# Weight splits and rotation tables on the Vector engine, squares of queries and keys summed on the Scalar engine

## The chip, the cores and the metric

The kernel runs on one core of one Trainium2 chip. The core has a matrix engine (PE), a Vector engine (DVE), a Scalar engine (ACT), a GpSimd engine (POOL) and a sync engine (SP) that issues the DMAs here. The metric is the device time of one execution in microseconds (us). Three runs of the kernel before gave a median of 1289.25 us (1287.78 to 1290.65).

## The reference, cut to what matters

Two layers work on 512 latent tokens and 256 context tokens of width 1024. Layer 0 is a pooling mixer and a squared-ReLU MLP, layer 1 is grouped-query attention (8 query heads, 4 key and value heads of width 128) and again an MLP. The change lies between the MLP of layer 0 and the attention of layer 1.

```python
def qkv_proj(h, w_qkv, q_g, k_g):
    B, L, _ = h.shape
    qkv = h @ w_qkv
    q, k, v = jnp.split(qkv, [N_HEADS * HEAD_DIM, (N_HEADS + N_KV_HEADS) * HEAD_DIM], axis=-1)
    q = rms_norm(q.reshape(B, L, N_HEADS, HEAD_DIM), q_g)
    k = rms_norm(k.reshape(B, L, N_KV_HEADS, HEAD_DIM), k_g)
    v = v.reshape(B, L, N_KV_HEADS, HEAD_DIM)
    return q, k, v

def attn_mix(h_ctx, h_lat, w_qkv, w_o, q_g, k_g, ctx_out):
    B, S, _ = h_lat.shape
    qc, kc, vc = qkv_proj(h_ctx, w_qkv, q_g, k_g)
    ql, kl, vl = qkv_proj(h_lat, w_qkv, q_g, k_g)
    tables = axial_rope_tables(S)
    ql = apply_axial_rope(ql, tables)
    kl = apply_axial_rope(kl, tables)
    ...
```

Each query and key head is divided by the root of the mean of its 128 squares (`rms_norm`), times a gain, and the latent ones are rotated by tables of cosines and sines. The kernel multiplies the gains into the tables once.

## The kernel before

**Numbers in two parts.** A matmul here takes a value as a rounded high part and a low part that holds the rest. `hilo` (L85) makes both: ACT copies the source into the high part (L86), and another engine subtracts that from the source into the low part (L87). A product is then three matmuls per block. `load_w` (L141) brings a 128x1024 block of weights into a buffer `raw` by a DMA on SP's queue and splits it into a tile `w` by `hilo`; its argument `lo_eng` says which engine makes the low part, DVE if nothing is given. The pool of `raw` has two buffers and the pool of `w` four, so a load waits until the split of the load two before has read its buffer, and a split waits until PE has done with the tile four before.

**The stage around the change.** The MLP of layer 0 ends in `m2_chunk` calls (L471): for each of 8 blocks of the width PE sums six matmuls (L490) in a PSUM tile `mm` (2 buffers) or `aux` (4 buffers), and DVE adds it, times a gate, to the stream `h_lat` (L348). The context comes first, then the two halves of the latent tokens; behind each part the squares of the stream are summed (L263, L266 on ACT, L267 on DVE), and PE, DVE (L284) and POOL (L286) make of them the factor 1/rms, which PE spreads (L297) and ACT copies (L304). `modulated` (L307) then gives the normalised input `a_m` (latent) and `a_c` (context) in two parts: DVE multiplies (L315), ACT or DVE scales and shifts (L319, L321), and `hilo` splits.

`ahead` (L839) loads the first two key weights `w_6335` and `w_6340` before the last blocks of the MLP are out; L999 loads the other two. The tables are four products `tabs` on POOL (L1007) of `angles` and `grow`, which come by DMA into two `raw` buffers.

For each of six tiles of 128 tokens (two of the context, four latent), `k_tile` (L886) multiplies the keys on PE (`project`, L860, 24 matmuls of 512 columns), then takes `inv_rms` (L862): ACT squares the PSUM tile (L865, 128x512), DVE sums each head (L867) and scales (L868), POOL raises to -0.5 (L870). `rotated` (L873) forms the rotated keys on DVE from PSUM and the tables (L879, L881, L883), DVE multiplies by the result of POOL (L898), PE turns the tile (L902), and `hilo` stores it as `k`. `q_steps` (L911) does the same for the queries, two tiles at a time with its own transpose (L926). Two of these come before the values (`v_tile`, L906) and six inside the attention loop (L1038), beside scores, softmax and the products with values and output weights.

**Order.** A scheduler places the instructions of each engine in one fixed row; an engine takes its own in that order and waits at the first that is not ready.

Of the kernel before, what the change touches and what calls it, by code (L numbers as in the profile page):

```python
# [10 lines left out]
AF = mybir.ActivationFunctionType  # L11
ALU = mybir.AluOpType
AX = mybir.AxisListType

P = 128
# [4 lines left out]
T = SEQ + CTX  # L20
# [3 lines left out]
HD = 128  # L24
# [23 lines left out]
def dit_block_kernel(ctx: ExitStack, tc: tile.TileContext, xT, cols, adab, adaw, w1, w2, wqkv, wo,  # L48
                     poolw, gvec, rope, edge, eye, out):
    nc = tc.nc  # L50
    act, dve, pool, pe = nc.scalar, nc.vector, nc.gpsimd, nc.tensor
# [22 lines left out]
    def new(p, shape, dt, tag, bufs=None):  # L74
        uid[0] += 1
        kw = {"bufs": bufs} if bufs else {}
        return p.tile(shape, dt, tag=tag, name=f"{tag}{uid[0]}", **kw)
# [7 lines left out]
    def hilo(hi, lo, src, lo_eng=dve):  # L85
        act.activation(hi, src, AF.Copy)  # L86
        lo_eng.tensor_tensor(lo, src, hi.bitcast(F32), op=ALU.subtract)  # L87
# [53 lines left out]
    def load_w(src, lo_eng=dve, ring=None, raw=None):  # L141

        t = new(wp, [P, 2, 1024], F32R, "w")
        if raw is None:
            raw = new(*(ring or (raws, [P, 1024], F32, "raw")))
            nc.sync.dma_start(raw, src)
        hilo(t[:, 0], t[:, 1], raw, lo_eng)
        return t
# [97 lines left out]
    def new_m(name, ctx_too=True):  # L246

        parts = [[big.tile([P, KT, SEQ], F32R, tag=t, name=f"{name}_{t}") for t in ("m_hi", "m_lo")]]
        if ctx_too:
            parts.append([[mc.tile([P, 4, CTX], F32R, tag="mc", name=f"{name}_c{x}{i}") for i in range(2)] for x in range(2)])  # L250
        return parts
# [87 lines left out]
    def run(*steps):  # L339
        steps = list(steps)  # L340
        while steps:
            step(steps)
# [14 lines left out]
    def m1_chunk(ws, outs, m, groups):  # L357

        n = max(c + n for rs in groups for c, n in rs)
        pss = []  # L360
        for _ in range(0, len(ws), 1024 // n):
            ps = ps_mm()
            pss.extend(ps[:, i * n : i * n + n] for i in range(1024 // n))
        for ranges in groups:
            for w, ps in zip(ws, pss):
                for k in range(KT):
                    for wx in range(2):
                        lhs = w[:, wx, k * P : k * P + P]
                        for ax in range(2 - wx):
                            for c0, cn in blocks_of(ranges):  # L370
                                pe.matmul(ps[:, c0 : c0 + cn], lhs, ms(m, ax, k, c0, cn),  # L371
                                          start=k + wx + ax == 0, stop=k == KT - 1 and wx == 1)
        m1_done(outs, pss)
# [123 lines left out]
    def mlp(i, m, total, last, first=None, between=None, ahead=None, strassen=None, acts=(), ws=()):  # L497
        gate = mod[i][:, 40:48]
        prev, acts, sides = None, list(acts), []
        for c in range(NCH):  # L500
            w2s = ()
            if prev is not None and 5 <= c < NCH - 1:
                w2s = [load_w(w2[i, 2 * c - 2 + t]) for t in range(2)]
            if not acts:
                several = 2 if first and c == 0 else 1
                acts = [new(ap_, [P, 2, 2, T], F32R, "act") for _ in range(several)]
                if strassen and c > 1 and c >= strassen[0]:
                    raw = strassen[2]()
                    for t in range(2):
                        nc.sync.dma_start(raw[:, t], w1[i, 2 * c + t])  # L510
                    m1_strassen(raw, inputs, acts[0], strassen[3], m if total > SEQ else None)
                    ws = ()
                else:
                    ws = ws or [load_w(w1[i, 2 * c + t]) for t in range(2 * several)]
                outs = [a[:, t] for a in acts for t in range(2)]
                if not ws:
                    pass
                elif several > 1:
                    m1_chunk(ws, outs, m, first)
                else:  # L520
                    for t in range(2):
                        m1_chunk(ws[t : t + 1], outs[t : t + 1], m, [[(0, total)]])
                ws = ()
            a = acts.pop(0)
            if between:
                between(c)
            if c == NCH - 1:
                break
            if strassen and c == 1:
                strassen = strassen(m)  # L530
                inputs, sides = strassen[1]
            if prev is not None:
                side = [sides.pop(0)] if sides else []
                m2_chunk(w2s or [load_w(w2[i, 2 * c - 2 + t]) for t in range(2)], prev, gate, [(0, total)], side)
                run(*side)
            prev = a

        wa, wb = ([load_w(w2[i, 2 * c + t]) for t in range(2)] for c in (NCH - 2, NCH - 1))
        (rng, each, after), rest = last[0], last[1:]
        m2_chunk(wa, prev, gate, [rng])  # L540
        m2_chunk(wb, a, gate, [rng], each=each)
        side = []
        m2_chunk(wa, prev, gate, [(rest[0][0][0], sum(r[1] for r, _, _ in rest))], side, [after], 2)
        if ahead:
            ahead()
        after = ()
        for n, (rng, each, then) in enumerate(rest):
            m2_chunk(wb, a, gate, [rng], side, after, each=each)
            after = [then]
        run(*side)  # L550
        return after
# [117 lines left out]
    for dt in range(8):  # L669
# [3 lines left out]
        if dt == KT - 1:  # L673
            ws = [load_w(w1[0, t]) for t in range(2)]
# [16 lines left out]
    m = new_m("m")  # L691

    units = [u for k in range(0, KT, 2) for u in ((0, k, 1), (0, k + 1, 1), (1, k, 2))]
    act0 = new(ap_, [P, 2, 2, T], F32R, "act")
# [40 lines left out]
    for u in range(len(units) + 2):  # L735
# [7 lines left out]
        if u == 1:  # L743
            last = ada0_products(9)
# [3 lines left out]
    ws = [load_w(w1[0, 2 + t]) for t in range(2)]  # L748
# [47 lines left out]
    def to_attn(c0, n):  # L796
        def place():
            if c0 not in spot:
                if c0 == SEQ:
                    spot[c0] = new(mc, [P, 2, 2, n], F32, "mc")  # L800
                else:
                    t = new(ap_, [P, 4, 2, n], F32, "act")
                    spot[0], spot[256] = t[:, :2], t[:, 2:]
            return spot[c0]

        def each(dt):
            if dt % 2:
                squares(place()[:, 0] if dt > 1 else None, dt - 1, 2, c0, n, place()[:, 0])

        def after():  # L810
            yield from norm_steps(1, 0, c0, n, lazy_m("a", True), place()[:, 0], place()[:, 1, 0])
        return (c0, n), each, after()

    last = [to_attn(SEQ, CTX), to_attn(0, 256), to_attn(256, 256)]
    kws = []
# [20 lines left out]
            return tile_of  # L836
        return STRASSEN_FROM[0], strassen_inputs(m, xs, (opp, "op"), (0, 1, 3)), lambda: new(rawp, [P, 2, 1024], F32, "pair"), op

    norm = mlp(0, m, T, last, between=between0, strassen=strassen0, acts=[act0], ws=ws, ahead=lambda: kws.extend(load_w(wqkv[u], pool) for u in range(2)))  # L839
    am_ = lazy_m("a", True)  # L840


# [7 lines left out]
    tabs = big.tile([P, 4, 4, HD], F32, tag="h_ctx", name="tabs")  # L850
# [11 lines left out]
    def inv_rms(x, n):  # L862

        sq = new(sc, [P, n, HD], F32, "sc")
        act.activation(sq, x, AF.Square)  # L865
        ss = new(sm, [P, n], F32, "sm8")
        dve.tensor_reduce(ss, sq, axis=AX.X, op=ALU.add)  # L867
        dve.tensor_scalar(ss, ss, 1.0 / HD, EPS, op0=ALU.mult, op1=ALU.add)  # L868
        rr = new(sm, [P, n], F32, "rr", 4)
        pool.tensor_tensor(rr, ss, neghalf[:, :n], op=ALU.pow)  # L870
        return rr
# [124 lines left out]
        return norm_steps(1, 1, c0, n, lazy_m("m2", False), bank=c0 > 0)  # L996

    TILES = (4, 5, 0, 1, 2, 3)
    ws = kws + [load_w(wqkv[u], (dve, pool)[u % 2]) for u in range(2, 4)]  # L999
    angles = new(raws, [P, 2, 4, HD], F32, "raw")  # L1000
    nc.sync.dma_start(angles, rope)
    grow = new(raws, [P, 4, HD], F32, "raw")
# [1 line left out]
    gk = const.tile([P, HD], F32, tag="gk", name="gk")  # L1004
    nc.sync.dma_start(gk, gvec[:, 2])
    for x in (2, 3, 0, 1):
        pool.tensor_tensor(tabs[:, x], angles[:, x % 2], grow[:, x].unsqueeze(1).to_broadcast([P, 4, HD]), op=ALU.mult)  # L1007
    def q_fill(g, ws):
        return [q_steps(ws, half, (g, half)) for half in range(2)]

# [8 lines left out]
            step(norm)  # L1019
    run(ks[4])  # L1020
    prev = ks[5]
    fill = q_fill(0, [load_w(wqkv[8 + u], pool) for u in range(2)])
    ws = []
    for n in range(2):
        next(fill[n])
        next(fill[n])
        run(prev)
        next(fill[n])
        prev = fill[n]
        ws.extend(load_w(wqkv[4 + 2 * n + u], pool) for u in range(2))  # L1030
    st, late, pend, wos = {}, [], [], None
    for n, tt in enumerate(TILES):
        v_tile(ws, tt)
# [3 lines left out]
    fill = []  # L1037
    for n in range(8 * NKV):  # L1038
        g, half, i = n // 8, n // 4 % 2, n % 4
        if i == 0 and half == 0 and g + 1 < NKV:  # L1040
            fill = q_fill(g + 1, [load_w(wqkv[8 + 2 * (g + 1) + u], pool) for u in range(2)])
# [22 lines left out]
        if i == 3:  # L1064
            prev, fill = fill[:1], fill[1:]
# [114 lines left out]
```

## Time and profile before

| | us |
|---|---|
| median of three runs | 1289.25 |
| the profiled execution, its own time | 1293.01 |
| its span in the profile | 1291.2 |
| PE busy in the span | 1247.2 (97%) |
| DVE busy | 1031.4 (80%) |
| ACT busy | 578.4 (45%) |
| POOL busy | 292.0 (23%) |

The profile records each instruction with its start and length, and what an idle engine waited for. Matmuls overlap and their ends are modelled, so the busy share of PE says when it had work, not how fast it was; the granted clock says that. Instructions on one engine overlap at their ends by some hundredths of a microsecond. Idle time of an engine that nobody waits for costs nothing.

### The profile page before, as it was taken

To read this page: it belongs to the slowest core of one execution; us is meant where nothing else is said; L and a number is where in the kernel's file an instruction comes from. 1 tells how busy PE (TensorE), PEld (TensorE's weight loads), DVE (VectorE), ACT (ScalarE), POOL (GpSimd) and SP (SyncE) were. 2 spreads that over 40 slices of the span, in tenths; PEclk is the share of its full clock that TensorE was granted. 3 is DMA by queue.
4 is the path that set the end of the run, shared out by engine and by line. 5 is a ranking of instruction groups with operands and counts; after the bars stand their busy time and mean duration, and the time that the engine had idled before them with its cause. 6 is when DMAs were issued, how large, how long until landed. Compare 5 with 4: busy or idle time off the path is not lost. (4 is left out here: it accounts for less than half of the span.)

```text
span 1291.2 us, 20478 instructions
## 1 busy us (share of the span) xinstructions
PE 1247.2 (97%) x8150; PEld 1107.8 (86%) x8150; DVE 1031.4 (80%) x1681; ACT 578.4 (45%) x954; POOL 292.0 (23%) x213
## 2 busy tenths in 40 slices
PE   6999999999999999999988999999989999999997
PEld 5567888899999999999877799999978898989896
DVE  6564998878989888766888377888889889898976
ACT  5445523444344443443343254545554544445443
POOL 0000000122221222230135122211030434343412
PEclk8999999999999999999989999999999999999998
DMA  9666414333434333302011011102213322222111
GB/s 349 268 254 220 139 66 159 104 114 115 147 115 147 117 128 117 129 34 66 33 58 66 33 66 34 65 34 66 82 66 114 131 98 98 99 98 99 66 34 66
DMA packets 41312, 138.68 MB, mean 107 GB/s; under 512 B 4736, under 2 KB 8064, under 8 KB 41088
## 3 DMA queue, kind: packets, MB, share of 16 engines
q1 hardware_dynamic: 41216, 137.36, 30.4%
q8 instruction: 64, 1.05, 0.3%
q14 instruction: 32, 0.26, 0.1%
HBM read 135.25 MB, written 2.10 MB: 106 GB/s over the span
## 5 line engine op out<-in xcount | busy, mean ns | idle before, releaser
L490 PE MATMUL aux<-act,w 128*128 128x512 f32 (+1 forms) x1224 | 240.0, 347 | 3.2 <-DVE h_lat L348 3.1
L490 PE MATMUL mm<-act,w 128*128 128x512 f32 (+1 forms) x1224 | 239.2, 347 | 0.6 <-DVE act L383 0.6
L490 PEld LDWEIGHTS aux<-act,w 128*128 128x128 f32 x1224 | 195.7, 189 | 32.7 <-DVE h_lat L348 3.9
L490 PEld LDWEIGHTS mm<-act,w 128*128 128x128 f32 x1224 | 196.2, 190 | 32.1 <-issue 1.7
L86 ACT ACTIVATE w<-raw 128x1024 fp32r<-128x1024 f32 x106 | 109.9, 1054 | 126.1 <-PE aux L490 90.7
L428 POOL TENSOR_TENSOR sc<-pair 128x512 f32<-128x512 f32 x55 | 77.7, 1422 | 320.6 <-DVE h_lat L348 107.5
L348 DVE SCALAR_TENSOR_TENSOR h_lat<-aux,mod,h_lat 128x512 f32<-128x512 f32 (+1 forms) x204 | 125.4, 628 | 16.5 <-PE aux L490 14.6
L428 POOL TENSOR_TENSOR sc<-fin 128x512 f32<-128x512 f32 x60 | 96.2, 1619 | 172.7 <-DVE r L448 83.6
L87 DVE TENSOR_TENSOR w<-raw,w 128x1024 fp32r<-128x1024 f32 x87 | 108.0, 1256 | 27.9 <-ACT w L86 27.5
L348 DVE SCALAR_TENSOR_TENSOR h_lat<-mm,mod,h_lat 128x512 f32<-128x512 f32 (+1 forms) x140 | 96.5, 697 | 6.7 <-PE mm L490 5.2
L371 PE MATMUL mm<-m_m_hi,w 128*128 128x512 f32 (+1 forms) x320 | 93.9, 356 | 1.0 <-ACT m_m_hi L86 1.0
L860 PE MATMUL aux<-w,a_m_hi 128*128 128x256 f32 (+1 forms) x384 | 88.2, 325 | 0.0
L219 DVE SCALAR_TENSOR_TENSOR mc<-raw,s_f,mc 128x512 f32<-128x512 f32 x112 | 83.4, 764 | 2.1 <-DMA raw<-in_dram 1.4
L439 PE MATMUL mm<-m_m_hi,mc 128*128 128x256 f32 x384 | 71.0, 283 | 0.0
L87 POOL TENSOR_TENSOR w<-raw,w 128x1024 fp32r<-128x1024 f32 x19 | 47.1, 2494 | 99.5 <-ACT w L86 99.5
L860 PEld LDWEIGHTS aux<-w,a_m_hi 128*128 128x128 f32 x384 | 64.7, 194 | 5.4
L371 PEld LDWEIGHTS mm<-m_m_hi,w 128*128 128x128 f32 x320 | 57.4, 194 | 11.2 <-ACT m_m_hi L86 1.2
L459 PE MATMUL aux<-m_c,w 128*128 128x256 f32 x528 | 65.2, 283 | 0.0
L459 PEld LDWEIGHTS aux<-m_c,w 128*128 128x128 f32 x528 | 64.2, 192 | 0.0
L467 DVE TENSOR_TENSOR act<-r,act 128x512 fp32r<-128x512 f32 x46 | 48.2, 1048 | 19.7 <-ACT r L466 19.7
L860 PE MATMUL aux<-w,a_m_lo 128*128 128x256 f32 (+1 forms) x192 | 62.1, 323 | 0.0
L439 PEld LDWEIGHTS mm<-m_m_hi,mc 128*128 128x128 f32 x384 | 60.7, 192 | 0.5
(245 smaller groups left out, 2575.1 us busy)
## 6 DMA issues: line engine op xcount, KB each, us to landing
raw<-in_dram SPq DMA_DIRECT2D x157, 512.0 KB, 3.3
praw<-in_dram SPq DMA_DIRECT2D x34, 512.0 KB, 8.0
fin<-in_dram SPq DMA_DIRECT2D x24, 512.0 KB, 4.1
pair<-in_dram SPq DMA_DIRECT2D x22, 512.0 KB, 4.3
block<-in_dram SPq DMA_DIRECT2D x8, 512.0 KB, 6.0
h_lat<-in_dram SPq DMA_DIRECT2D x4, 512.0 KB, 7.0
w<-in_dram SPq DMA_DIRECT2D x4, 512.0 KB, 11.7
out_dram<-fin SPq DMA_DIRECT2D x8, 256.0 KB, 2.5
```

The costliest lines, as they stand in the source:

```text
L86: act.activation(hi, src, AF.Copy)
L87: lo_eng.tensor_tensor(lo, src, hi.bitcast(F32), op=ALU.subtract)
L219: dve.scalar_tensor_tensor(acc[:, s], w, scal, acc[:, s], op0=ALU.mult, op1=ALU.add)
L348: dve.scalar_tensor_tensor(h, ps, gate[:, dt, s : s + 1], h, op0=ALU.mult, op1=ALU.add)
L371: pe.matmul(ps[:, c0 : c0 + cn], lhs, ms(m, ax, k, c0, cn), start=k + wx + ax == 0, stop=k == KT - 1 and wx == 1)
L428: pool.tensor_tensor(t, x, y, op=how)
L439: pe.matmul(places[n], w[:, wx, k * P : k * P + P], inputs[n][ax][:, k], start=k + wx + ax == 0, stop=k == 3 and wx == 1)
L459: pe.matmul(pc[:, t * 256 : t * 256 + 256], ws[k // 4][:, wx, k % 4 * P : k % 4 * P + P], ms(m, ax, k, SEQ, CTX), start=k + wx + ax == 0, ...
L467: dve.tensor_tensor(lo, r, hi.bitcast(F32), op=ALU.subtract)
L490: pe.matmul(ps, lhs, a[:, t, ax, c0 : c0 + n], start=t + wx + ax == 0, stop=t == 1 and wx == 1)
L860: pe.matmul(ps, lhs, ws[u][:, wx, o : o + width], start=k + ax + wx == 0, stop=k == KT - 1 and ax == 1)
```

## The change

Four calls of `load_w` lose their argument `pool`, so that DVE makes the low parts of nine weight blocks in this stage: two key weights in `ahead`, one of the two in L999 (the other was with DVE already), two query weights and four value weights. The four products of the tables go from POOL to DVE. In `inv_rms` the one squaring of 128x512 and the sum over each head on DVE give way to four squarings of 128x128 on ACT, each with an accumulator output that gives the sum of its head; this holds for all 14 tiles of keys and queries. The split of the weights in the attention loop stays where it was, in part on POOL. From L867 on the numbers of the lines are those of before; L867 is now the squaring.

```diff
-    norm = mlp(0, m, T, last, ..., ahead=lambda: kws.extend(load_w(wqkv[u], pool) for u in range(2)))
+    norm = mlp(0, m, T, last, ..., ahead=lambda: kws.extend(load_w(wqkv[u]) for u in range(2)))
...
     def inv_rms(x, n):
         sq = new(sc, [P, n, HD], F32, "sc")
-        act.activation(sq, x, AF.Square)
         ss = new(sm, [P, n], F32, "sm8")
-        dve.tensor_reduce(ss, sq, axis=AX.X, op=ALU.add)
+        for i in range(n):
+            act.activation(sq[:, i], x[:, i], AF.Square, accum_out=ss[:, i : i + 1])
         dve.tensor_scalar(ss, ss, 1.0 / HD, EPS, op0=ALU.mult, op1=ALU.add)
...
-    ws = kws + [load_w(wqkv[u], (dve, pool)[u % 2]) for u in range(2, 4)]
+    ws = kws + [load_w(wqkv[u]) for u in range(2, 4)]
...
     for x in (2, 3, 0, 1):
-        pool.tensor_tensor(tabs[:, x], angles[:, x % 2], grow[:, x].unsqueeze(1).to_broadcast([P, 4, HD]), op=ALU.mult)
+        dve.tensor_tensor(tabs[:, x], angles[:, x % 2], grow[:, x].unsqueeze(1).to_broadcast([P, 4, HD]), op=ALU.mult)
...
-    fill = q_fill(0, [load_w(wqkv[8 + u], pool) for u in range(2)])
+    fill = q_fill(0, [load_w(wqkv[8 + u]) for u in range(2)])
...
-        ws.extend(load_w(wqkv[4 + 2 * n + u], pool) for u in range(2))
+        ws.extend(load_w(wqkv[4 + 2 * n + u]) for u in range(2))
```

Three places show how DVE's row changes. The first is DVE at the end of the MLP of layer 0, where the last block of 512 tokens (`aux_6327`) is added and the blocks of 256 follow (`mm_6345` is the first of them); before:

```order
L348 SCALAR_TENSOR_TENSOR h_lat<-aux_6327,mod_134,h_lat 128x512
L348 SCALAR_TENSOR_TENSOR h_lat<-mm_6345,mod_134,h_lat 128x256
L87 TENSOR_TENSOR a_c_6250<-sc_6313,a_c_6248 128x512
L348 SCALAR_TENSOR_TENSOR h_lat<-mm_6353,mod_134,h_lat 128x256
L348 SCALAR_TENSOR_TENSOR h_lat<-aux_6363,mod_134,h_lat 128x256
```

The same place on DVE in the changed kernel:

```order
L348 SCALAR_TENSOR_TENSOR h_lat<-aux_6327,mod_134,h_lat 128x512
L87 TENSOR_TENSOR w_6335<-raw_6336,w_6335 128x1024
L87 TENSOR_TENSOR a_c_6250<-sc_6313,a_c_6248 128x512
L87 TENSOR_TENSOR w_6340<-raw_6341,w_6340 128x1024
L348 SCALAR_TENSOR_TENSOR h_lat<-mm_6345,mod_134,h_lat 128x256
L348 SCALAR_TENSOR_TENSOR h_lat<-mm_6353,mod_134,h_lat 128x256
```

Two splits of key weights now stand between the last large block and the first small one. The second place is DVE where the first key tiles meet the norm of the second half of the latent tokens (`sm_6599`, in the changed kernel `sm_6601`, is its variance); before:

```order
L315 TENSOR_TENSOR sc_6524<-h_lat,act_6361 128x512
L867 TENSOR_REDUCE sm_6586<-sc_6584 128x4
L87 TENSOR_TENSOR a_m_lo<-sc_6518,a_m_hi 128x2x256
L321 TENSOR_SCALAR sc_6524<-sc_6524,am_139,mod_135 128x256
L868 TENSOR_SCALAR sm_6586<-sm_6586 128x4
L897 TENSOR_TENSOR sc_6591<-aux_6559,gk 128x512
L87 TENSOR_TENSOR a_m_lo<-sc_6524,a_m_hi 128x2x256
L898 TENSOR_TENSOR sc_6591<-sc_6591,rr_6589 128x512
L284 TENSOR_SCALAR sm_6599<-mm_6594 128x2
L897 TENSOR_TENSOR sc_6638<-aux_6606,gk 128x512
```

The same place on DVE in the changed kernel:

```order
L315 TENSOR_TENSOR sc_6524<-h_lat,act_6361 128x512
L87 TENSOR_TENSOR w_6544<-raw_6545,w_6544 128x1024
L87 TENSOR_TENSOR a_m_lo<-sc_6518,a_m_hi 128x2x256
L321 TENSOR_SCALAR sc_6524<-sc_6524,am_139,mod_135 128x256
L284 TENSOR_SCALAR sm_6601<-mm_6596 128x2
L87 TENSOR_TENSOR a_m_lo<-sc_6524,a_m_hi 128x2x256
L1007 TENSOR_TENSOR tabs<-raw_6549,raw_6551 128x512 x4
L868 TENSOR_SCALAR sm_6585<-sm_6585 128x4
L897 TENSOR_TENSOR sc_6593<-aux_6559,gk 128x512
L898 TENSOR_TENSOR sc_6593<-sc_6593,rr_6591 128x512
```

The variance of the second half (L284) now comes ahead of the first key tile instead of inside it, a split stands ahead of it and the four tables behind it. The third place is DVE in the key tile of the latent tokens 256 to 383 (its product is `aux_6757`, in the changed kernel `aux_6765`); before:

```order
L879 TENSOR_TENSOR sc_6796<-aux_6757,tabs 128x512
L881 TENSOR_TENSOR sc_6797<-aux_6757,tabs 128x4x64 x2
L883 TENSOR_TENSOR sc_6796<-sc_6796,sc_6797 128x512
L898 TENSOR_TENSOR sc_6796<-sc_6796,rr_6794 128x512
L867 TENSOR_REDUCE sm_6837<-sc_6835 128x4
```

The same place on DVE in the changed kernel:

```order
L879 TENSOR_TENSOR sc_6806<-aux_6765,tabs 128x512
L881 TENSOR_TENSOR sc_6807<-aux_6765,tabs 128x4x64 x2
L87 TENSOR_TENSOR w_6868<-raw_6869,w_6868 128x1024
L883 TENSOR_TENSOR sc_6806<-sc_6806,sc_6807 128x512
L87 TENSOR_TENSOR w_6873<-raw_6874,w_6873 128x1024
L898 TENSOR_TENSOR sc_6806<-sc_6806,rr_6804 128x512
```

The splits of the two query weights came in between the steps of the tile, and the reduction went. Behind the attention every engine's row is as before, and so is SP's row from the first instruction to the last.

## Rows read from the trace of the kernel before

**Rows 1.** Busy time of the engines in two stretches, the stage of the change and the attention loop (columns: stretch and its length; busy us and instructions of PE, PE's weight loads, DVE, ACT, POOL; granted clock; DMA).

```profile
630.00:720.00 90.00, 77.14 (x433) 66.75 (x432) 75.46 (x114) 36.09 (x56) 40.66 (x27) 0.94 0.20 68
720.00:920.00 200.00, 195.15 (x1427) 182.57 (x1426) 151.35 (x319) 94.80 (x181) 34.73 (x29) 1.00 0.13 43
```

**Rows 2.** Timeline of PE in the stage (start, length, instruction; in brackets the idle time ahead of it and who ended it).

```profile
632.45 2.32 PE L490 MATMUL aux<-act,w 128*128 128x256 f32 x18
...
637.84 0.38 PE L490 MATMUL aux<-act,w 128*128 128x256 f32 x1 [3.08 <-DVE h_lat L348]
638.24 0.98 PE L490 MATMUL mm<-act,w 128*128 128x256 f32 x6
...
653.77 2.79 PE L860 MATMUL aux<-w,a_c 128*128 128x512 f32 x11 [1.16 <-DVE w L87]
...
657.21 5.29 PE L860 MATMUL aux<-w,a_c 128*128 128x512 f32 x22
...
667.09 1.23 PE L297 MATMUL mm<-ident,sm 128*128 128x128 f32 x4 [3.23 <-POOL sm L286]
...
695.64 0.63 PE L902 MATMUL aux<-ident,sc 128*128 128x128 f32 x4 [2.62 <-DVE sc L898]
...
703.81 0.63 PE L902 MATMUL aux<-ident,sc 128*128 128x128 f32 x4 [1.79 <-DVE sc L898]
...
715.93 1.43 PE L860 MATMUL aux<-w,a_c 128*128 128x512 f32 x5 [0.97 <-POOL w L87]
```

**Rows 3.** PE alone in short stretches (columns: stretch and length, PE busy and matmuls, granted clock, DMA share and GB/s).

```profile
639.00:643.00 4.00, 4.00 (x23) 0.57 0.15 61
664.00:667.00 3.00, 0.00 (x0) 0.91 0.68 233
667.00:673.30 6.30, 6.21 (x17) 0.50 0.14 57
695.60:702.00 6.40, 6.36 (x52) 1.00 0.33 115
```

**Rows 4.** Timeline of DVE in the stage.

```profile
609.06 1.22 DVE L87 TENSOR_TENSOR w<-raw,w 128x1024 fp32r<-128x1024 f32 x1
...
632.32 2.46 DVE L87 TENSOR_TENSOR a_c<-sc,a_c 128x512 fp32r<-128x512 f32 x1
634.70 2.42 DVE L321 TENSOR_SCALAR sc<-sc,am,mod 128x256 f32<-128x256 f32 x1
637.05 0.74 DVE L348 SCALAR_TENSOR_TENSOR h_lat<-aux,mod,h_lat 128x512 f32<-128x512 f32 x1
637.71 0.47 DVE L348 SCALAR_TENSOR_TENSOR h_lat<-mm,mod,h_lat 128x256 f32<-128x256 f32 x1
638.10 0.68 DVE L87 TENSOR_TENSOR a_c<-sc,a_c 128x512 fp32r<-128x512 f32 x1
...
666.04 0.15 DVE L284 TENSOR_SCALAR sm<-mm 128x2 f32<-128x2 f32 x1
```

**Rows 5.** Timeline of POOL in the stage.

```profile
631.82 5.16 POOL L87 TENSOR_TENSOR w<-raw,w 128x1024 fp32r<-128x1024 f32 x2 [8.46 <-ACT w L86]
...
657.45 6.47 POOL L1007 TENSOR_TENSOR tabs<-raw,raw 128x512 f32<-128x512 f32 x4 [4.82 <-DMA raw<-in_dram]
...
669.61 1.38 POOL L870 TENSOR_TENSOR rr<-sm,neghalf 128x4 f32<-128x4 f32 x1 [2.58 <-DVE sm L868]
678.86 1.01 POOL L870 TENSOR_TENSOR rr<-sm,neghalf 128x4 f32<-128x4 f32 x1 [7.87 <-DVE sm L868]
```

**Rows 6.** Groups of DVE's and POOL's instructions between 630 and 720 us, shapes kept apart (columns: line, engine, operation, tiles and shapes, count; busy us, mean ns of one; idle time before).

```profile
L883 DVE TENSOR_TENSOR sc<-sc,sc 128x512 f32<-128x512 f32 x6 | 9.9, 1654 | 0.1
L898 DVE TENSOR_TENSOR sc<-sc,rr 128x512 f32<-128x512 f32 x6 | 8.1, 1346 | 1.2 <-POOL rr L870 0.9
L321 DVE TENSOR_SCALAR sc<-sc,am,mod 128x256 f32<-128x256 f32 x10 | 7.9, 803 | 0.0
L867 DVE TENSOR_REDUCE sm<-sc 128x4 f32<-128x512 f32 x8 | 5.4, 679 | 4.1 <-ACT sc L865 4.1
L87 DVE TENSOR_TENSOR w<-raw,w 128x1024 fp32r<-128x1024 f32 x1 | 3.4, 3426 | 0.0
...
L87 POOL TENSOR_TENSOR w<-raw,w 128x1024 fp32r<-128x1024 f32 x9 | 22.9, 2553 | 10.8 <-ACT w L86 10.8
```

**Rows 7.** Groups of ACT's instructions between 600 and 1000 us: copies of 384 and 256 columns from PSUM, the squaring, and the reading of an accumulator.

```profile
L86 ACT ACTIVATE act<-aux 128x384 fp32r<-128x384 f32 x64 | 28.0, 490 | 7.4 <-PE aux L961 7.4
L865 ACT ACTIVATE sc<-aux 128x512 f32<-128x512 f32 x14 | 8.3, 591 | 14.7 <-PE aux L860 14.7
L86 ACT ACTIVATE mc<-aux 128x256 fp32r<-128x256 f32 x16 | 6.1, 384 | 7.8 <-PE aux L974 7.7
L946 ACT ACTIVATION_READ_ACCUMULATOR r<-mm,nb,sr 128x1 f32 x32 | 6.1, 191 | 0.0
```

**Rows 8.** Timeline of ACT around an exponential with an accumulator output.

```profile
744.14 0.98 ACT L946 ACTIVATE r<-mm,nb,sr 128x768 f32<-128x768 f32 x1
745.01 0.19 ACT L946 ACTIVATION_READ_ACCUMULATOR r<-mm,nb,sr 128x1 f32 x1
745.11 1.05 ACT L86 ACTIVATE w<-raw 128x1024 fp32r<-128x1024 f32 x1
```

**Rows 9.** The DMA of `grow` (columns: issue, count, KB, us from issue to landing).

```profile
raw<-in_dram SPq DMA_DIRECT2D x1, 256.0 KB, 3.6
```

More of the change, by code (lines that the diff above doesn't have):

```diff
@@ L837, in strassen0 @@
         return STRASSEN_FROM[0], strassen_inputs(m, xs, (opp, "op"), (0, 1, 3)), lambda: new(rawp, [P, 2, 1024], F32, "pair"), op
-    norm = mlp(0, m, T, last, between=between0, strassen=strassen0, acts=[act0], ws=ws, ahead=lambda: kws.extend(load_w(wqkv[u], pool) for u in range(2)))
+    norm = mlp(0, m, T, last, between=between0, strassen=strassen0, acts=[act0], ws=ws, ahead=lambda: kws.extend(load_w(wqkv[u]) for u in range(2)))
     am_ = lazy_m("a", True)
```

## The prediction

> **What bounds the kernel now.** I read the stretches first. PE is the bound: in the attention loop it idles 4.85 of 200 us [rows 1], so work taken off the other engines there buys little. In the stage between 630 and 720 us it has work for 77.14 of 90 us, and DVE is nearly full with 75.46 us [rows 1]. So I went to PE's timeline there: it stops six times, for 3.08, 1.16, 3.23, 2.62, 1.79 and 0.97 us, 12.85 us in all [rows 2]. Four of the stops are ended by DVE, one by POOL's split, and one by POOL's L286, which itself follows DVE's L284 at 666.04 [rows 2, 4].
>
> The stops cost more than their length. Behind the one of 3.08 us PE had a granted clock of 0.57 for 4 us; behind the one of 3.23 us it had 0.50, the 1.2 GHz level, for 6.2 us of work [rows 3]. Time lost to that: 4.0 x 0.43 = 1.7 us and 6.21 x 0.50 = 3.1 us, together 4.8 us. Behind the stop of 2.62 us the clock stayed at 1.00 (2.4 GHz) [rows 2, 3].
>
> Why is DVE late? Its own instructions stretch. POOL's first two splits run from 631.82 to 636.98 us [rows 5]; in that time DVE's `a_c` split takes 2.46 instead of 0.68 us and an L321 2.42 us, and both end within 0.4 us behind an end of one of POOL's two [rows 4, 5]. The addition of the block that PE waits for comes after them, at 637.05, and PE's stop of 3.08 us ends with it [rows 2, 4]. The same shows in the groups: against 0.68 us of a free instruction of that shape [rows 4], L883 loses 6 x 0.97 = 5.8 us and L898 6 x 0.67 = 4.0 us; the one weight split that DVE has takes 3.43 instead of 1.22 us, 2.2 more [rows 4, 6]. With the first two (1.8 and, at 0.40 us for a free L321 as an estimate from half the columns of the 0.68, 2.0), that is 15.8 us of DVE lost behind POOL.
>
> **The change part by part.** *Splits.* POOL loses nine of 2.55 us, 22.9 us [rows 6], DVE gets nine of 1.22 us, 11.0 us [rows 4]. *Tables.* POOL loses 6.47 us [rows 5], DVE gets four of about 0.68 us, 2.7 us. *Reductions.* DVE loses eight of 0.68 us in the stage, 5.4 us [rows 6]. DVE in the stage: 11.0 + 2.7 - 5.4 - 15.8 = -7.5 us. So DVE gets emptier although it gets more work, if POOL is what stretched it.
>
> *Squares.* Per tile ACT gives up 0.59 us. From 512, 384 and 256 columns at 0.59, 0.49 and 0.38 us [rows 7], each 128 columns cost 0.106 us, so 128 columns take about 0.28 us, an estimate. An instruction with an accumulator is followed by a read of 0.19 us, which begins 0.11 us before the first has ended and lets the next begin after 0.10 us [rows 8]. If the four overlap like that: 4 x (0.28 - 0.11 + 0.10) = 1.08 us; if nothing overlaps: 4 x (0.28 + 0.19) = 1.88 us. I take 1.08, since rows 8 show just this pair. ACT's step grows by 0.5 to 1.3 us and DVE's 0.68 us goes out of the same chain, so the chain from product to turned tile changes by -0.2 to +0.6 us. What hides it is that PE works at the next tile meanwhile, 24 matmuls at 5.29 / 22 = 0.24 us, 5.8 us [rows 2].
>
> Against such a cut stands a rule of the Trainium skill, page "VectorE: DVE Perf Modes", section "The TRN2 errata": instructions pay a fixed cost each, so one wants 512 elements or more in one. Its figure for ACT from PSUM, 172 cycles plus the elements at 1.2 GHz, gives 250 ns for 128 and 570 ns for 512, as an estimate; the rows (0.28 and 0.59) agree. Four of 250 ns and four reads in a row would be 1.76 us, inside my two ends, and the sum stays.
>
> *First place of the order.* The block of `aux_6327` is added before the two new splits now. From 632.32: `a_c` 0.68, L321 0.40, the addition 0.74, each starting some 0.08 us before the one before it ends (632.32 + 2.46 is 634.78, the next starts at 634.70 [rows 4]): it is done at 633.9, before PE has run out of other work at 632.45 + 2.32 = 634.8 [rows 2]. The stop of 3.08 us goes. Next is late what stands behind the splits: 1.22 + 0.68 + 1.22 + 0.47 us less the overlaps puts the first small block at 637.2 us. PE has six more matmuls ready (`aux_6409`, 0.16 us each at most, rows 2), so it stops from about 635.5 to 637.3: **a new wait of 1.8 us**. Bounds: 0 if the buffers hold out longer, 2.4 without the overlaps. The longer stop of 2.62 us left the clock alone [rows 2, 3], so I charge no slow stretch.
>
> *Second place.* With `w_6539` split in 1.22 instead of 3.43 us and no waits ahead, the norm of the first half is some 5 us earlier. L284 of the second half comes before the first key tile instead of inside it. By the lengths in rows 4 I place it at 655.7 us; to PE's start of L297 it took 1.05 us before (666.04 to 667.09 [rows 2, 4]), and PE gets there only at about 658.5. The stop of 3.23 us goes, and its slow stretch. Behind it DVE holds the four tables until `grow` has come: its DMA is free to start when `w_6544` is split, about 654.7, and takes 3.6 us [rows 9], so to 658.3; DVE stands still some 1.3 us, and behind it wait the first two key tiles and the second half of `a_m`. PE asks for the first of these after tile 0, at about 664; the first key tile is ready near 662.8. This cover is 1 us.
>
> *Third place.* Two splits of query weights stand between the steps of a key tile; they add 2.4 us where the lock added up to 1.0 + 0.7 us per step pair on average [rows 6]. The weights' buffers come free in the tile of PE behind this one, and one such tile lasts 5.8 us, so both splits and L898 are done about when PE gets there: cover 0.3 us. The same holds for the next pair with a cover of 0.6. The stops of 2.62 and 1.79 us go, and so does 0.97, since the low part no longer takes 2.5 us on POOL. For the thin covers at these places I charge 0.8 us.
>
> *Loop.* Six more query tiles trade the reduction for the four squarings; PE idles 4.85 us there in all [rows 1]. I take 0, with -0.6 to +2.
>
> **The sum**, on the profiled execution (1293.01 us, 3.8 above the median, of which 1.8 lies outside its span of 1291.2): -12.85 - 4.8 + 1.8 + 0.8 = -15.05 us, 1278.0 us there. The stops stand in the program and not in the profiler, so I take the same from the median: 1289.25 - 15.05 = **1274.2 us**.
>
> **The rivals.** *DVE becomes the bound.* The seven splits behind the first two stand in DVE's row ahead of steps that PE wants. For it speaks the thin cover; against it that DVE's stage gets emptier by 7.5 us. If each holds PE for its whole 1.22 us, 8.5 us come back: 1282.7; for half, 1278.5. A slow clock behind the new stop of 1.8 us (3.1 us as in rows 3) lies in the same range.
>
> By the Trainium skill, page "SBUF — State Buffer", section "Who interferes with whom", DVE and POOL share a pair of ports that whoever starts first holds for its whole instruction, so DVE's splits could hold up POOL's powers too. The trace has one such: 1.38 instead of 1.01 us [rows 5]. By the rule eight powers could lose up to 1.2 us each, and the time would lie in the range of this rival.
>
> *Slower.* One mechanism: the squarings do not overlap, and the longer chain reaches PE at every tile. Price: 14 x (1.88 - 0.59) = 18.1 us, more than the 15.05 gained: 1292.3 us. It decides from 15.05 / 14 = 1.1 us per tile on PE's path. Against it: PE is a tile of 5.8 us ahead, and the reduction of 0.68 us leaves the chain.
>
> *It doesn't do what it says.* DVE's stretched instructions have another cause than POOL; then the stops stay, and the gain is nil or within 2.6 us: 1286.6 to 1291.8. Against it: the ends that fall together [rows 4, 5].
>
> **How the numbers follow.** Forecast (gain of 11 to 18 us, 1271 to 1278): 0.65. DVE bound (1278 to 1286.6): 0.24. No change: 0.05. Slower: 0.06. The low end is the forecast without the new stop and the 0.8, and 0.6 from the loop: 1271.0. The high end takes in two thirds of the DVE rival: 1282.5. A measurement of this kernel can tell about 0.2% (2.6 us) from no change. Faster by more: 0.89; within: 0.05; slower by more: 0.06.
>
> **What would show it.** Right: in the stage L883 and L898 near 0.68 us; the stops of 3.08, 3.23, 2.62 and 1.79 us gone; one new stop near 1.8 us behind the blocks of 512; granted clock 1.00 throughout; the squaring with its read near 0.27 us per head. Wrong: stops of PE ended by DVE's weight splits or by the tables, a stretch at 1.2 GHz, or DVE's instructions still stretched, which would leave POOL out as the cause.

## The result, and the profile of the changed kernel

| | before | changed |
|---|---|---|
| median of six runs, us | 1288.78 (1287.7 to 1290.65) | 1277.21 (1276.13 to 1278.6) |
| the profiled execution, own time | 1293.01 | 1278.06 |
| its span | 1291.2 | 1275.9 |
| mean granted clock in the span | 0.987 | 0.993 |

The ratio is 0.991, with a 95% interval of 0.9897 to 0.9923: the change takes 11.6 us off the median. The two profiled executions differ by 15.0 us, of which more in the section on the prediction.

Stretches of the changed kernel, the stage and the attention loop (columns as in [rows 1]; the stage is shorter now, so the cuts lie 15 us earlier):

```profile
630.00:705.00 75.00, 72.68 (x438) 64.18 (x437) 63.33 (x118) 39.69 (x112) 12.04 (x14) 1.00 0.25 81
705.00:905.00 200.00, 192.29 (x1417) 180.08 (x1416) 150.05 (x312) 97.08 (x220) 33.92 (x29) 1.00 0.13 43
```

In the stage PE idles 2.3 of 75 us, where it idled 12.9 of 90 [rows 1]. In the loop it idles 7.7 of 200 us, where it idled 4.85 [rows 1]: something was given back there. PE's timeline in the stage has two stops left:

```profile
631.52 3.04 PE L490 MATMUL aux<-act,w 128*128 128x256 f32 x24
636.38 1.70 PE L490 MATMUL mm<-act,w 128*128 128x256 f32 x12 [1.82 <-DVE h_lat L348]
...
681.77 0.63 PE L902 MATMUL aux<-ident,sc 128*128 128x128 f32 x4 [0.49 <-DVE sc L898]
```

The first is the new one, behind the two early splits. The row of DVE there shows every instruction at its free length, the addition in front of the splits and the small blocks behind them:

```profile
631.39 0.69 DVE L87 TENSOR_TENSOR a_c<-sc,a_c 128x512 fp32r<-128x512 f32 x1
631.99 0.41 DVE L321 TENSOR_SCALAR sc<-sc,am,mod 128x256 f32<-128x256 f32 x1
632.31 0.75 DVE L348 SCALAR_TENSOR_TENSOR h_lat<-aux,mod,h_lat 128x512 f32<-128x512 f32 x1
632.98 1.22 DVE L87 TENSOR_TENSOR w<-raw,w 128x1024 fp32r<-128x1024 f32 x1
634.11 0.69 DVE L87 TENSOR_TENSOR a_c<-sc,a_c 128x512 fp32r<-128x512 f32 x1
634.71 1.22 DVE L87 TENSOR_TENSOR w<-raw,w 128x1024 fp32r<-128x1024 f32 x1
635.85 0.87 DVE L348 SCALAR_TENSOR_TENSOR h_lat<-mm,mod,h_lat 128x256 f32<-128x256 f32 x2
```

Groups of DVE's instructions in the stage, 630 to 705 us, against those of [rows 6] (columns as there, with lines left out):

```profile
L87 DVE TENSOR_TENSOR w<-raw,w 128x1024 fp32r<-128x1024 f32 x10 | 12.2, 1221 | 1.9 <-ACT w L86 1.9
...
L898 DVE TENSOR_TENSOR sc<-sc,rr 128x512 f32<-128x512 f32 x6 | 4.1, 691 | 0.6 <-POOL rr L870 0.5
L883 DVE TENSOR_TENSOR sc<-sc,sc 128x512 f32<-128x512 f32 x6 | 4.1, 689 | 0.1
...
L321 DVE TENSOR_SCALAR sc<-sc,am,mod 128x256 f32<-128x256 f32 x10 | 4.0, 410 | 0.0
```

L883 fell from 1654 to 689 ns and L898 from 1346 to 691. DVE's busy time in the stage, from 623.5 to 717.2 us before and from 622.6 to 700.1 us in the changed kernel, fell from 80.4 to 68.5 us. ACT's four squarings of a tile, with their reads:

```profile
657.22 0.28 ACT L867 ACTIVATE sc<-aux 128x128 f32<-128x128 f32 x1 [1.58 <-PE aux L860]
657.40 0.19 ACT L867 ACTIVATION_READ_ACCUMULATOR sc<-aux 128x1 f32 x1
657.49 0.27 ACT L867 ACTIVATE sc<-aux 128x128 f32<-128x128 f32 x1
...
658.14 0.22 ACT L867 ACTIVATION_READ_ACCUMULATOR sc<-aux 128x1 f32 x1
```

From 657.22 to 658.36 is 1.14 us per tile; 1.08 was expected. Last, the loop in the changed kernel, with PE first (its two longest stops), then DVE and POOL at the first of them:

```profile
767.24 1.01 PE L961 MATMUL aux<-ident,r 128*128 128x128 f32 x6 [1.67 <-DVE mc L87]
...
817.44 1.01 PE L961 MATMUL aux<-ident,r 128*128 128x128 f32 x6 [1.61 <-DVE mc L87]
...
763.92 2.35 DVE L868 TENSOR_SCALAR sm<-sm 128x4 f32<-128x4 f32 x1 [3.34 <-ACT sc L867]
766.18 0.68 DVE L879 TENSOR_TENSOR sc<-aux,tabs 128x512 f32<-128x512 f32 x1
766.78 0.41 DVE L87 TENSOR_TENSOR mc<-aux,mc 128x256 fp32r<-128x256 f32 x1
...
761.50 4.74 POOL L87 TENSOR_TENSOR w<-raw,w 128x1024 fp32r<-128x1024 f32 x2 [18.02 <-ACT w L86]
```

and the same place in the kernel before (DVE, then POOL):

```profile
780.53 0.69 DVE L867 TENSOR_REDUCE sm<-sc 128x4 f32<-128x512 f32 x1 [2.79 <-ACT sc L865]
781.13 0.68 DVE L879 TENSOR_TENSOR sc<-aux,tabs 128x512 f32<-128x512 f32 x1
781.73 0.41 DVE L87 TENSOR_TENSOR mc<-aux,mc 128x256 fp32r<-128x256 f32 x1
...
778.65 4.76 POOL L87 TENSOR_TENSOR w<-raw,w 128x1024 fp32r<-128x1024 f32 x2 [17.40 <-ACT w L86]
```

Both times POOL splits two weights. Before, the reduction stood at that place and took its 0.69 us in the middle of POOL's pair. Now the scaling of four numbers per row (L868) stands there and ends with POOL's pair, at 766.27 against 766.24; L879 and the low part `mc` that PE waits for come behind it. This happens to two of the six L868 of the loop (2.35 us here, 2.34 at 814.1). The kernel before has one such case, where L868 stands behind L879; DVE, POOL and PE there:

```profile
877.43 2.04 DVE L868 TENSOR_SCALAR sm<-sm 128x4 f32<-128x4 f32 x1
...
877.06 2.38 POOL L87 TENSOR_TENSOR w<-raw,w 128x1024 fp32r<-128x1024 f32 x1 [15.38 <-ACT w L86]
...
880.27 0.84 PE L961 MATMUL aux<-ident,r 128*128 128x128 f32 x6 [1.01 <-DVE sc L881]
```

So the trace of before already showed that such a step can stretch beside POOL and hold PE, there for 1.01 us.

**Where the time went.** I measure, on the profiled executions, the stage from the first L297 behind the context's blocks to the second L926 (the first matmul of each group), and the loop from there to the next L297:

| | stage | loop |
|---|---|---|
| before | 93.71 | 201.48 |
| changed | 77.56 | 204.13 |

The stage gains 16.15 us and the loop gives 2.65 back; with 0.9 each ahead of the stage and behind the loop, where the rows of both kernels are the same, this is the difference of the spans, 15.3.

### The profile page after: what moved, and what is told of

Read it like the earlier page. It is cut to its first block, busy times and chain, and to the rows that moved or that the text cites. A ratio compares the mean times of both kernels' runs of the same rounds, so it can differ in the third digit from the quotient of the medians.

```text
span 1275.9 us, 20565 instructions
## 1 busy us (share of the span) xinstructions
PE 1238.5 (97%) x8150; PEld 1102.5 (86%) x8150; DVE 1020.1 (80%) x1680; ACT 585.7 (46%) x1052; POOL 261.4 (20%) x200
## 5 line engine op out<-in xcount | busy, mean ns | idle before, releaser
L87 DVE TENSOR_TENSOR w<-raw,w 128x1024 fp32r<-128x1024 f32 x96 | 116.9, 1232 | 28.4 <-ACT w L86 27.9
L371 PE MATMUL mm<-m_m_lo,w 128*128 128x512 f32 (+1 forms) x160 | 56.3, 352 | 1.6 <-DVE m_m_lo L87 1.6
```

The costliest lines, as they stand in the source:

```text
L371: pe.matmul(ps[:, c0 : c0 + cn], lhs, ms(m, ax, k, c0, cn), start=k + wx + ax == 0, stop=k == KT - 1 and wx == 1)
```

## The experiments

Times are medians, ratios against the runs of before on the same chip, with 95% intervals; stage and loop are measured as above, each on one profiled execution.

| run | us | ratio | stage | loop |
|---|---|---|---|---|
| splits alone | 1281.74 | 0.9936 (0.9917 to 0.9956) | 85.10 | 201.44 |
| squares alone | 1293.61 | 1.003 (1.0016 to 1.0043) | 94.25 | 205.39 |
| squared whole in the loop | 1275.25 | 0.9889 (0.9869 to 0.9908) | 77.50 | 201.65 |
| loop's splits on DVE | 1270.95 | 0.986 (0.9837 to 0.9883) | 77.54 | 198.55 |
| POOL reads beside | 1290.41 | 0.9995 (0.9986 to 1.0005) | 88.82 | 204.03 |
| POOL only writes beside | 1278.97 | 0.9914 (0.99 to 0.9929) | 78.21 | 203.95 |
| second split later | 1279.13 | 0.9915 (0.9902 to 0.9929) | 78.58 | 203.99 |
| squares twice | 1282.25 | 0.9942 (0.9929 to 0.9954) | 79.76 | 205.49 |
| loop on DVE, split later | 1272.84 | 0.9868 (0.9855 to 0.9882) | 78.75 | 198.47 |
| loop on DVE, whole in it | 1274.47 | 0.9879 (0.9862 to 0.9895) | 79.01 | 200.63 |

The theory: POOL's splits lengthened DVE's instructions, and these made PE stop. The rivals: DVE had too much work, and the reductions' leaving is the gain; or PE waited for POOL's late results.

**POOL reads beside.** Behind each of the nine high parts POOL subtracts it from itself into a place that is free.

```diff
         hilo(t[:, 0], t[:, 1], raw, lo_eng)
+        if lock:
+            hi = t[:, 0].bitcast(F32).rearrange("p (x c) -> p x c", x=2)
+            pool.tensor_tensor(dump[0], hi, hi, op=ALU.subtract)
```

> The changed kernel with nine more instructions on POOL alone: behind each high part of the nine weight blocks POOL subtracts it from itself (128x1024, as the old split) into a place nobody reads. The rows of all other engines are the same, word for word, and nobody waits for the nine. Theory (POOL's instructions stretch DVE's by being there): DVE's instructions of 0.69 us in the stage last up to 2.5 us again and PE's stops come back, with a slow clock behind the longer ones: 1284 to 1294 us. Rival (it was POOL's lateness, or DVE's order, that made PE wait; POOL busy beside costs nothing): 1277 to 1278.5 us.

The gain is gone, to within 0.1% of before, although the stage is not all the way back: 88.82 us, where the kernel before had 93.71 and the changed one has 77.56. Nobody waits for the nine, and the rows of DVE, PE, ACT and SP are those of the changed kernel. Here is one place of it, POOL, DVE and PE (L888 and L907 are L883 and L902 of the changed kernel):

```profile
683.77 4.72 POOL L150 TENSOR_TENSOR v<-w 128x1024 fp32r<-128x1024 f32 x2
...
683.82 2.92 DVE L87 TENSOR_TENSOR w<-raw,w 128x1024 fp32r<-128x1024 f32 x1
686.66 2.38 DVE L888 TENSOR_TENSOR sc<-sc,sc 128x512 f32<-128x512 f32 x1
...
690.92 1.09 PE L907 MATMUL aux<-ident,sc 128*128 128x128 f32 x4 [3.90 <-DVE sc L903]
```

DVE loses 1.7 us on each of the two, and PE stops for 3.90 us; behind it the granted clock was 0.74 for 6.1 us. So POOL's presence alone brings stops back with the rows of the other engines unchanged: POOL's late results are not needed for it, and DVE's amount of work is the same as in the changed kernel. What the 4.9 us are that did not come back is not shown; the stop of 0.97 us that POOL's own split ended [rows 2] could be a part.

**POOL only writes beside.** The same place, but POOL fills it with zeros, twice, behind a copy of one column by ACT.

```diff
+        if lock:
+            act.activation(dump[0][:, 0, :1], t[:, 0, :1], AF.Copy)
+            for _ in range(2):
+                pool.memset(dump[0].bitcast(F32), 0.0)
```

> As the run with nine more subtractions on POOL, but in place of each subtraction POOL fills the same place with zeros twice (128x1024, it reads nothing from SBUF); a copy of one column by ACT in front keeps it behind the high part. The rows of PE, DVE and SP are the same. Theory (it is POOL's reading that holds DVE's instructions with two operands in SBUF): DVE keeps its 0.69 us, 1277 to 1280 us, up to 2 us of it for the nine small copies on ACT. Rival (any POOL instruction that touches SBUF holds DVE): DVE's instructions beside the fills stretch by the length of a fill, 1284 us or more.

The fills take POOL 17.7 us (nine pairs of 1.96 to 1.99), the nine subtractions took it 20.6, and the time is within 1.8 us of the changed kernel's. Groups of DVE, first where POOL reads, then where it only writes (630 to 715 and 630 to 706 us):

```profile
L903 DVE TENSOR_TENSOR sc<-sc,rr 128x512 f32<-128x512 f32 x6 | 5.8, 970 | 0.6 <-POOL rr L875 0.5
L888 DVE TENSOR_TENSOR sc<-sc,sc 128x512 f32<-128x512 f32 x6 | 5.8, 968 | 0.1
```

```profile
L904 DVE TENSOR_TENSOR sc<-sc,rr 128x512 f32<-128x512 f32 x6 | 4.1, 686 | 0.6 <-POOL rr L876 0.5
L889 DVE TENSOR_TENSOR sc<-sc,sc 128x512 f32<-128x512 f32 x6 | 4.1, 685 | 0.1
```

L889 at 679.52 us lay wholly beside fills and took 0.68 us. It is POOL's reading that holds DVE's additions and products of two tiles in SBUF: the instruction that also reads does it, the one that only writes does not. The Trainium skill, page "SBUF — State Buffer", section "Who interferes with whom", says this: a DVE instruction with two SBUF inputs contends with a GpSimd instruction that reads SBUF and not with one that only writes. The two runs agree, with 970 and 686 ns.

**One half of the change at a time.** Splits and tables alone (the diff's lines on `load_w` and L1007):

> The kernel before with the nine splits and the tables on DVE, the squares as before (one squaring of 512 columns, DVE sums the heads). Theory (POOL's splits stretch DVE's instructions and so make the stops of PE; the squares are beside the point and give a little back in the attention loop): the gain is all here, 1274.5 us (1273 to 1276.5) where the whole change gives 1277.2, and in the loop DVE's small L868 lies outside POOL's splits again. Rival (the reductions must leave DVE for the splits to fit): eight reductions of 0.68 us stand in the stage's row again, 5.4 us, the stops of PE between key tiles come back and the time is 1280 us or more.

Squares alone (the diff's lines in `inv_rms`):

> The kernel before with only the squares changed (four squarings of 128 columns with accumulator outputs, no reduction on DVE). Theory: the long instructions of DVE and the six stops of PE stay, since POOL's splits stay: 1289 us (1287 to 1292), with about 2 us given back in the loop. Rival (the reductions filled DVE and the change's gain is 5.4 us taken off it): 1284 us or less. Rival of the prediction (unoverlapped squarings reach PE): 1295 us or more.

My theory was wrong on the first: 1281.74 us and not 1274.5. On the second, 1293.61 us lies above its range (1287 to 1292) and below the rival's 1295. The halves give -8.0 and +3.9 us, together -4.1, and the change gives -11.6. With the splits alone PE's stops in the stage, besides the first of 1.81 us, are these (what lies between them is left out):

```profile
661.98 0.71 PE L297 MATMUL mm<-ident,sm 128*128 128x128 f32 x4 [0.73 <-POOL sm L286]
...
674.15 0.33 PE L902 MATMUL aux<-ident,sc 128*128 128x128 f32 x1 [0.53 <-DVE sc L898]
...
684.31 0.63 PE L902 MATMUL aux<-ident,sc 128*128 128x128 f32 x4 [2.15 <-DVE sc L898]
...
688.48 0.58 PE L860 MATMUL aux<-w,a_m_hi 128*128 128x256 f32 x1 [1.36 <-DVE w L87]
```

DVE works for 28.45 of 30 us between 660 and 690 there, with its instructions at free length, and PE for 25.22; in the changed kernel DVE for 26.94 and PE for 29.50. The clock fell behind each of the last two (PE alone, columns as in [rows 3]):

```profile
684.30:686.70 2.40, 2.39 (x16) 0.76 0.15 58
688.50:695.00 6.50, 6.50 (x40) 0.70 0.48 161
```

So the forecast's rival that DVE becomes the bound is what happens when the reductions stay, in that rival's range, and the reductions' leaving is worth 7.5 us of stage beside the splits (85.10 to 77.56), 4.3 of it in stops and, from the two rows above, some 2.5 in the clock (2.39 x 0.24 + 6.50 x 0.30). Without the splits it is worth nothing there (94.25 against 93.71): POOL's splits still set the stops, five of them with 12.1 us in place of six with 12.85. The squares alone are slower, and the loss is the loop's 3.9 us: some 1.5 of it the clock behind the stage's last stop (0.72 for the loop's first 5.4 us), the rest about what the changed kernel gives back there.

**What the loop lost.** The six query tiles of the loop squared whole again, the stage as changed:

```diff
-        rr = inv_rms(ps.rearrange("p (n c) -> p n c", n=4), 4)
+        rr = inv_rms(ps.rearrange("p (n c) -> p n c", n=4), 4, key[0] > 0)
```

> The changed kernel, but the 6 query tiles inside the attention loop are squared whole and summed by DVE as before; the stage keeps everything of the change. Theory (with the reductions gone the scheduler puts DVE's L868 of 128x4 where a POOL split runs, and it waits 2.4 us for it, which holds PE 1.0 us twice and more): the loop gets back what it lost, 2.0 to 2.7 us, so 1274.5 to 1275.2. Rival (the loss in the loop is chance of the order or lies in MLP 2): within 1 us of 1277.2.

Or the loop's remaining splits taken from POOL:

```diff
-            fill = q_fill(g + 1, [load_w(wqkv[8 + 2 * (g + 1) + u], pool) for u in range(2)])
+            fill = q_fill(g + 1, [load_w(wqkv[8 + 2 * (g + 1) + u]) for u in range(2)])
...
-            wos = [load_w(wo[2 * g + j], (dve, pool)[j]) for j in range(2)]
+            wos = [load_w(wo[2 * g + j]) for j in range(2)]
```

> The changed kernel, with the weight splits in the attention loop that were still POOL's (two query weights and one output weight per round) on DVE too. Theory (what the loop loses is POOL's splits holding DVE): DVE's long instructions in the loop go, as in the stage, and the time is 1273.5 to 1275.5. Rival (in the loop, where PE idles least, DVE's longer row is what counts): each split costs PE up to its 1.22 us, the time is 1278 to 1286.

The first gives the loop back 2.5 of its 2.65 us; the medians differ by 2.0, with intervals that overlap, so the loop's length carries this. The second keeps the squares head by head and still makes the loop 5.6 us shorter, 2.9 shorter than in the kernel before; its 1270.95 us lies below the range that I expected (1273.5 to 1275.5). L868 in the loop, 720 to 920 us, before, changed, and with the loop's splits on DVE:

```profile
L868 DVE TENSOR_SCALAR sm<-sm 128x4 f32<-128x4 f32 x6 | 2.8, 473 | 0.0
```

```profile
L868 DVE TENSOR_SCALAR sm<-sm 128x4 f32<-128x4 f32 x6 | 5.4, 895 | 14.4 <-ACT sc L867 14.4
```

```profile
L868 DVE TENSOR_SCALAR sm<-sm 128x4 f32<-128x4 f32 x6 | 1.0, 169 | 6.6 <-ACT sc L867 6.6
```

So the loss was DVE's small step falling into POOL's splits, and not ACT's longer one by itself. Both remedies together, with the loop's splits on DVE and its tiles squared whole:

> The changed kernel with the loop's splits on DVE (1270.95 us by itself) and the six query tiles of the loop squared whole and summed by DVE again, which by itself took 2.0 us off the changed kernel. Theory (head by head costs the loop only because DVE's 128x4 step then falls into POOL's splits, and those are gone here): nothing to win, and DVE's row has six reductions of 0.68 us more: 1271 to 1274 us. Rival (the longer step on ACT is itself what the loop pays for): 1268.5 to 1269.5 us.

1274.47 us, half a microsecond above the range, and the loop is 2.1 us longer than with the squares head by head: with POOL out of the way the reductions are only DVE's extra work. The stage is 1.5 us longer here too (79.01), though up to the loop all rows and stops are those of the changed kernel. What differs is the clock behind the stop of 1.83 us. First PE's stop in this run, then the stretch behind it, then the same stretch in the changed kernel (columns as in [rows 3]):

```profile
633.15 1.78 PE L490 MATMUL mm<-act,w 128*128 128x256 f32 x12 [1.83 <-DVE h_lat L348]
```

```profile
634.00:640.00 6.00, 6.00 (x40) 0.72 0.26 83
```

```profile
637.00:643.00 6.00, 6.00 (x53) 1.00 0.27 87
```

**The chain on ACT.** Each tile's squarings made twice, the second overwriting the first (the loop over the heads inside `for _ in range(2):`).

> The changed kernel with each tile's four squarings made twice, the second overwriting the first: ACT's step grows by another 1.0 us per tile, 14 us in all. Theory (ACT's step lies beside the product of the next tile): 1277 to 1280 us. Rival of the prediction (the chain of squares reaches PE at every tile): 1289 us or more.

1282.25 us, 5.0 more than the changed kernel for 14 us more of ACT, between the two expectations. In the stage 2.2 us come out, with a stop of 1.86 us at the place where 0.49 was: the cover there is thin, but most tiles hide a second round. Parts of PE's and DVE's rows stand in another order in this run, and a stop of 1.85 us in the loop was followed by a granted clock of 0.51 for 3.5 us, so not all of the 5.0 us need be the squares.

**The stop that is left.** The second early split with a lower priority, alone and with the loop's splits on DVE:

```diff
-        lo_eng.tensor_tensor(lo, src, hi.bitcast(F32), op=ALU.subtract)
+        with tc.high_priority(offset=-later) if later else ExitStack():
+            lo_eng.tensor_tensor(lo, src, hi.bitcast(F32), op=ALU.subtract)
```

> The changed kernel with a lower priority for the low part of the second early key weight, so that it stands behind the small blocks at the end of the MLP and no longer ahead of them. Theory (the one stop left of 1.82 us is the two splits ahead of the first small block): the stop falls to 0.6 us or less and the time by 1.2 to 1.8: 1275.4 to 1276. Rival (the stop is held by the block's own sums, or the later split holds its raw buffer and the next weights are late): 1277 us or more, with a stop elsewhere.

> The changed kernel with the splits in the attention loop on DVE too (1270.95 us by itself) and the second early split later. Theory: the two gains add, 1269.2 to 1270 us. Rival: the later split gives nothing or takes from the key tiles, 1271 us or more.

Neither gains. PE's stops of the first of them:

```profile
633.20 1.69 PE L491 MATMUL mm<-act,w 128*128 128x256 f32 x12 [0.69 <-DVE h_lat L349]
...
644.13 0.71 PE L298 MATMUL mm<-ident,sm 128*128 128x128 f32 x4 [0.84 <-POOL sm L287]
...
680.77 0.63 PE L903 MATMUL aux<-ident,sc 128*128 128x128 f32 x4 [1.25 <-DVE sc L899]
```

The stop falls from 1.82 to 0.69 as expected, but the moved rows put 0.84 us ahead of the first half's norm and 0.76 more at a key tile; the stage is 1.0 us longer. The medians against the kernels without the edit (1279.13 to 1277.21, 1272.84 to 1270.95) are 1.9 us higher, with intervals that overlap. The fastest kernel of the study is the changed one with the loop's splits on DVE, 1270.95 us.

## Why the prediction was right, and where it was off

The forecast was 1274.2 us in a range of 1271.0 to 1282.5; 1277.2 came.

*Right: the cause.* POOL's splits stretch DVE; the run with POOL reading beside shows it. DVE's instructions went to their free lengths, as said. DVE's work in the stage fell by 11.9 us though it took on nine splits and four tables; 7.5 was forecast. With the terms for splits, tables and reductions as they stood (+8.3), the stretching was worth some 20 us and not 15.8, since I had left out L315, the low parts of `a_m` and all but one L321.

*Right: the stops.* Of 12.85 us [rows 2] 2.31 are left, so 10.5 are gained; the forecast was 12.85 - 1.8 - 0.8 = 10.25. The new stop is 1.82 us and the thin covers cost 0.49. L284 of the second half came at 654.82 (655.7 was expected), and DVE stood still for 0.51 us ahead of the tables (1.3). No stop was ended by the tables or by a split in the stage's later part.

*Right for the profile, too large for the median: the clock.* The step that was mis-sized is "The stops stand in the program and not in the profiler, so I take the same from the median". The stops do, but what the clock does behind them differs from run to run. The clock's loss in the stage was 4.8 us in the profile of before and nothing in that of the changed kernel, as forecast. But the same stop need not have the same clock behind it: 1.83 us were followed by 0.72 in the run with the loop's splits on DVE and whole squares, and 1.82 by 1.00 in the changed kernel, on the same rows; and the stop of 2.62 us, with 1.00 behind it in the kernel before [rows 3], comes again with the squares alone, and has this behind it:

```profile
693.15 0.63 PE L902 MATMUL aux<-ident,sc 128*128 128x128 f32 x4 [2.62 <-DVE sc L898]
```

```profile
693.15:700.00 6.85, 6.85 (x45) 0.75 0.31 101
```

So that I charged no slow stretch behind the new stop was right for this profile by luck; in that other run the stage was 1.5 us longer for it. In 17 runs of before on one chip the mean granted clock of the span lay between 0.985 and 0.993 and the time between 1285.78 and 1292.53 us; the four runs at 0.991 or more have a median of 1287.5, the six at 0.987 or less one of 1291.2. The changed kernel's six runs were all at 0.992 or 0.993. The profiled execution of before stood at 0.987, the median one of the 17 at 0.989. By the distance to 0.993, 0.006 for the one and 0.004 for the other, the term of -4.8 shrinks to about 4.8 x 4 / 6 = 3.2 for the median, 1.6 less; this is an estimate. Where the slow stretches lie in runs without a trace was not seen. The prediction had the sign before it: the profiled execution was 3.8 us above the median. It put 1.8 of that down to the time outside the span, but every run has that time (the median one of the 17 took 1289.7 us with a span of 1287.9), so all 3.8 were this execution's own.

*Wrong: the loop.* I took 0, with -0.6 to +2; it was +2.65. I priced the squarings by PE's idle time and did not ask what DVE's row would hold beside POOL's remaining splits. The reduction had been standing there, untouched; its place fell to L868, whose 0.17 us became 2.35, twice in the loop, with 1.67 and 1.61 us of PE's time. The L868 at 877.43 in the kernel before was the warning.

With both the sum is -10.5 - 0.8 - 3.2 + 2.65 = -11.9 us; 11.6 was measured. The 0.8 is what remains of the stage (16.15 - 10.5 - 4.8); it lies in PE's busy time, since the stops make up all of PE's idle time there, and I can't place it. Between the two profiled executions 15.0 us came, 3.4 more than between the medians: 1.6 by the estimate for the clock, and 1.8 ahead of the stage and behind the loop, where the rows did not change.

*The range.* Its high end was to take in two thirds of the rival of a full DVE (1278 to 1286.6), but 1282.5 lies about half way.

*The rivals.* That DVE becomes the bound did not come, but only because the reductions left with the splits; I had counted them in DVE's sum without saying that the forecast hangs on them. That POOL's powers are held up did not come either: the eight in the stage took 1.01 to 1.04 us each. But none of them began beside a split of DVE's. The one small instruction of POOL that did, the scaling L919 at 697.51 us beside a split at 697.47, took 1.27 us instead of 0.23; PE did not stop for it. The longer chain of squares did not reach PE, and its double cost 5 of 14 us.

## What to carry to other kernels

Before work is moved from a full engine's neighbour to the full engine, look at whether the neighbour makes it full: DVE's instructions that end with POOL's are the sign, and taking POOL's reads away can empty DVE more than the moved work fills it. Then ask of every instruction that changes its place which of those still fall beside POOL, since a step of four columns can cost as much as a whole split. Where a term of the sum is the clock, weigh it by the mean clock of the runs and not by that of one profiled run.

## What was not expected of the hardware

- A `TENSOR_SCALAR` of 128x4 took 2.35 us beside POOL's splits (2.04 once in the kernel before) and 0.17 us without. A `TENSOR_REDUCE` of 128x512 took its 0.69 us in the middle of such splits, and so did instructions with one operand in PSUM (L879, 0.68 us). Of the reduction the same section of the Trainium skill says that it never contends; the row at 780.53 agrees.
- Fills on POOL, which read nothing, left `TENSOR_TENSOR` alone, but the two L321 beside them took 1.09 and 0.59 instead of 0.41 us; PE's first stop was 2.28 us there and not 1.82.
- One subtraction of 128x1024 on POOL took 2.00 us beside a DVE split that took 2.91; two in a row beside two of DVE's took 4.72, and DVE's 2.92 and 2.38. They went in turns.
- With the splits alone a stop of 2.15 us was followed by a granted clock of 0.76, where one of 2.62 us in the kernel before was followed by 1.00 [rows 2, 3]. On the same rows a stop of 1.82 us was followed by 1.00 in one execution and one of 1.83 by 0.72 in another. What sets the difference is open.
